# GLA on one Trainium2 core: both directions' states stacked into one 128-row product, decay factors made three levels ahead, decayed queries loaded per chunk

## The chip, the core and the metric

The kernel runs on one core of one Trainium2 chip. A core has a matrix engine (TensorE: PE in the rows, its weight loads PEld), a vector engine (VectorE: DVE), a scalar engine (ScalarE: ACT), GpSimd (POOL) and SyncE (SP), whose queue issues most DMA transfers. The engines run side by side, each through its own instructions in a fixed order, and wait for one another by semaphores. Products are written to PSUM, which POOL does not read. The metric is the device time of one execution in microseconds; the median of three runs counts.

## The reference, cut to what matters

One step of a network of two mixer layers over 2,048 latent positions and 128 context positions, all in float32. The change is in the first layer's gated linear attention (GLA): 4 heads with keys of 64 and values of 128, run forwards and backwards over the positions.

```python
def gla_chunked(q, k, v, g, s0):
    ...
    def step(S, inp):
        qc, kc, vc, gc = inp
        b = jnp.cumsum(gc, axis=2)
        o_inter = jnp.einsum('bhcd,bhde->bhce', qc * jnp.exp(b), S)
        diff = b[:, :, :, None, :] - b[:, :, None, :, :]
        decay = jnp.where(causal, jnp.exp(jnp.where(causal, diff, 0.0)), 0.0)
        att = jnp.einsum('bhid,bhjd,bhijd->bhij', qc, kc, decay)
        o = o_inter + jnp.einsum('bhij,bhje->bhie', att, vc)
        b_last = b[:, :, -1:, :]
        S_new = jnp.exp(b_last)[:, :, 0, :, None] * S + jnp.einsum('bhcd,bhce->bhde', kc * jnp.exp(b_last - b), vc)
        return S_new, o
    ...
def gla_bidir(q, k, v, gf, gb, s0f, s0b):
    o_f, s_f = gla_chunked(q, k, v, gf, s0f)
    fl = lambda t: jnp.flip(t, axis=2)
    o_b, s_b = gla_chunked(fl(q), fl(k), fl(v), fl(gb), s0b)
    return o_f + fl(o_b), s_f, s_b
```

The GLA output is normalised per head, gated, put beside the output of the layer's second branch (S5), projected by `w_out`, and added to the input; the sum is normalised again for the second layer.

## The kernel before

The positions are 17 chunks of 128: 16 latent ones (0 to 15) and the context (16). The program is written in Python and a list scheduler fixes the order of every engine's instructions when it is built; that order, the pools of buffers and the PSUM banks decide who waits for whom.

The backward states need a pass from the last chunk to the first. `gla_back` makes it in an earlier stage, between products of other kinds: for each chunk it loads keys, cumulated gates `B` and values, decays the keys, transposes them and multiplies them with the values in `kv_update`, whose four products (one a head) lie in turn in the left and the right 64 columns of the array. Two DVE operations then write the next state into `sb`, which keeps all sixteen backward states on the chip. The pass that closes this stage, `glu_pass`, ends the S5 branch; its stores of `ys_d` and those of `zg_d` stand on POOL's queue.

Stage 4 (`phase4`) does the GLA chunks. `weave` runs four generators round by round: `gla_chunk(i)`, `turn(i-1)` (gates and transposes the previous chunk's output), `gla_pre(i+1)` (prepares the next chunk) and `after(i-2)` (output projection of 96 products, residual, norm for the next layer, transposes in `make_h`). The scheduler orders what they emit.

Within a chunk the decay is split by seven levels of distance (`STEPS` 64 to 1). For each, `gla_arg` has POOL subtract gates in four operations (the lines 980 to 983), ACT take the exponential, and DVE multiply with queries and keys (the tile `arg`); PE multiplies the pair head by head with 64 rows (L1058), and DVE merges the result into `att` under a mask (L1065). Levels 0 and 1 have two buffers, later ones four. `gla_pre` makes levels 0 to 2, and `gla_chunk` makes level `li+2` when it uses level `li`. Then PE makes the output of each head: forward state product (L1073, 64 rows), backward state product (L1074, 64 rows), attention product (L1075, 128 rows), accumulated in one bank of `psP`:

```python
if i < 16:
    nc.tensor.matmul(ot, qh[o : o + 64, 0, pr, :], sf[o : o + 64, pr], start=True, stop=False)
    nc.tensor.matmul(ot, qh[o : o + 64, 1, pr, :], self.sb[o : o + 64, i, pr], start=False, stop=False)
nc.tensor.matmul(ot, att[:, hh, pr], v[:, h * 128 : h * 128 + 128], start=i == 16, stop=True)
```

A float32 product takes two passes through the array, and shows as two instructions in the rows. The decayed queries `qh` are made on the chip from `B` and `qk`.

Of the kernel before, what the change touches and what calls it, by code (L numbers as in the profile page):

```python
# [48 lines left out]
class Kernel:  # L49
# [55 lines left out]
    def setup(self, es):  # L105
# [33 lines left out]
        self.b_d = d.tile([2, 2, 128, NT], F32, name="b_d")  # L139
        self.z_d = d.tile([16, 512, 137], F32, name="z_d")  # L140
# [749 lines left out]
    def gla_back(self, es):  # L890
# [3 lines left out]
        for i in [16] + list(range(15, 0, -1)):  # L894
# [11 lines left out]
            kv = self.kv_update(p, E, v)  # L906
            if i == 16:
                st = p.tile([128, 2, 128], F32, name="bst", tag="bst", bufs=1)
                nc.scalar.copy(st, kv)
                nc.sync.dma_start(self.o["gla"][1].rearrange("r p v -> p r v"), st)  # L910
# [30 lines left out]

    def gla_setup(self, es):
# [16 lines left out]
        self.gp = self.pool(es, "glap", 2, side="right")  # L959
        self.gs = {}  # L960
# [3 lines left out]
    def gla_arg(self, i, li):  # L964
# [10 lines left out]
        arg = self.ga["arg"][li > 1].tile([128, 2, 256], F32, name="arg", tag="arg", bufs=4 if li > 1 else 2)  # L975
# [12 lines left out]
    def gla_pre(self, i):  # L988
# [32 lines left out]
        sf = st["sf"] = self.sf  # L1021
        if i != 15:
            kv = self.kv_update(p, kh, v)
            if i == 16:
                o = p.tile([128, 2, 128], F32, name="fst", tag="sf", bufs=3)
                nc.scalar.copy(o, kv)
                nc.sync.dma_start(self.o["gla"][0].rearrange("r p v -> p r v"), o)
            else:
                self.sf = p.tile([128, 2, 128], F32, name="sf", tag="sf", bufs=3)
                for pr in range(2):  # L1030
                    V.scalar_tensor_tensor(self.sf[:, pr], sf[:, pr], eb[:, pr : pr + 1], kv[:, pr], op0=OP.mult, op1=OP.add)
        yield

    def gla_chunk(self, i, out):
# [4 lines left out]
        v, qh, sf = st["v"], st["qh"], st["sf"]  # L1039
# [736 lines left out]
```

## Time and profile before

| what | value |
|---|---|
| median of three runs | 2424.79 us (2420.01 to 2428.99) |
| the profiled execution: time, span | 2423.86 us, 2422.1 us |
| busy share of the span | PE 95%, PEld 87%, DVE 71%, ACT 41%, POOL 36% |
| mean granted TensorE clock | 0.971 of full |
| stage 4, first GLA product to last output copy | 908.8 to 1335.2 us of the span |

The profile covers one execution. Its span runs from the first to the last instruction; 1.8 us lie around it. Busy shares are means over stages that have different limits, so the stage of the change is read by itself. A granted clock of 1.00 is TensorE's upper level (2.4 GHz), 0.50 the lower (1.2 GHz); a value between is a mean over a stretch with both.

### The profile page before, as it was taken

What the parts mean: (1) busy time and instruction counts of PE and PEld (TensorE: products, weight loads), DVE (VectorE), ACT (ScalarE), POOL (GpSimd) and SP (SyncE); (2) the same over time, 40 slices, a digit from 0 to 9 for tenths busy, and PEclk for the clock granted to TensorE, in tenths of its full rate; (3) what the DMA queues carried; (4) which work ended last, traced back from release to release, by engine and by line L of the source; (5) the groups of instructions that cost most, each with busy time, mean ns of one, the idle gap of its engine ahead of it and who ended that gap; (6) DMA issues with size and microseconds to landing.
All of it is one profiled execution on the core that took longest, in us unless ns stands there. A gap on an engine that the chain in (4) does not pass through costs nothing.

```text
span 2422.1 us, 47150 instructions
## 1 busy us (share of the span) xinstructions
PE 2295.5 (95%) x17521; PEld 2110.7 (87%) x17521; DVE 1720.3 (71%) x3932; ACT 986.2 (41%) x2365; POOL 872.9 (36%) x1328
## 2 busy tenths in 40 slices
PE   7998998999999986999999999999999998999998
PEld 4987887777787875888888999999999997999998
DVE  5998689999976776888888675556344336676765
ACT  4553532222244453445554532233122115565653
POOL 4017047777612227666765022211001102222221
PEclk9999999999999995989999999999999998999999
DMA  8442552233269873333433642245124213222221
GB/s 303 153 141 79 170 159 78 80 82 96 81 202 315 294 242 112 122 105 114 124 118 99 192 135 79 79 134 169 50 73 122 68 56 113 88 88 88 89 70 57
DMA packets 313174, 303.92 MB, mean 125 GB/s; under 512 B 43696, under 2 KB 264464, under 8 KB 312944
## 3 DMA queue, kind: packets, MB, share of 16 engines
q1 hardware_dynamic: 255072, 227.70, 31.6%
q10 hardware_dynamic: 48112, 42.38, 5.4%
q0 software_dynamic: 9760, 30.83, 3.5%
q8 instruction: 138, 2.26, 0.4%
q14 instruction: 92, 0.75, 0.1%
HBM read 212.43 MB, written 88.39 MB: 124 GB/s over the span
## 4 chain that ended last, share of the span: by engine, by line
PE 53%; DVE 7%; issue 5%; DMA 4%; POOL 2%; ACT 2%; SPq 0%; ACTq 0%; POOLq 0%; DVEq 0%
PE psW L100 7%; PE psW L102 7%; PE psW L101 7%; PE psD L100 6%; PE psD L102 6%; PE psD L101 6%; PE psW L1487 2%; PE psW L1440 2%; PE psT L1475 2%; PE psP L1058 2%; PE psP L1075 1%; PE psP L1073 1%; DVE hq L1065 1%; DVE arg L985 1%; DVE yT L1103 1%
## 5 line engine op out<-in xcount | busy, mean ns | idle before, releaser
L100 PE MATMUL psD<-slot,yT 128*128 128x256 f32 x1088 | 316.4, 292 | 2.4 <-ACT yT L1102 2.4
L102 PE MATMUL psD<-slot,yT 128*128 128x256 f32 x1088 | 314.0, 292 | 0.4 <-DVE yT L1103 0.4
L101 PE MATMUL psD<-slot,yT 128*128 128x256 f32 x1088 | 311.2, 287 | 0.0
L101 PE MATMUL psW<-hq,slot 128*128 128x272 f32 x1024 | 293.0, 288 | 0.0
L102 PE MATMUL psW<-hq,slot 128*128 128x272 f32 x1024 | 292.9, 287 | 0.0
L100 PE MATMUL psW<-hq,slot 128*128 128x272 f32 x1024 | 289.1, 287 | 0.0
L101 PE MATMUL psD<-hq,slot 128*128 128x272 f32 x768 | 227.8, 297 | 14.5 <-DVE hq L230 14.5
L100 PE MATMUL psD<-hq,slot 128*128 128x272 f32 x768 | 230.0, 301 | 9.4 <-ACT fo L791 8.2
L102 PE MATMUL psD<-hq,slot 128*128 128x272 f32 x768 | 228.5, 298 | 0.0
L100 PEld LDWEIGHTS psD<-slot,yT 128*128 128x128 f32 x1088 | 208.0, 191 | 9.9 <-ACT yT L1102 2.8
L101 PEld LDWEIGHTS psD<-slot,yT 128*128 128x128 f32 x1088 | 208.1, 191 | 2.1
L102 PEld LDWEIGHTS psD<-slot,yT 128*128 128x128 f32 x1088 | 205.7, 191 | 4.3 <-issue 1.3
L102 PEld LDWEIGHTS psW<-hq,slot 128*128 128x128 f32 x1024 | 193.1, 189 | 0.0
L101 PEld LDWEIGHTS psW<-hq,slot 128*128 128x128 f32 x1024 | 192.5, 188 | 0.0
L100 PEld LDWEIGHTS psW<-hq,slot 128*128 128x128 f32 x1024 | 190.6, 188 | 0.0
L101 PEld LDWEIGHTS psD<-hq,slot 128*128 128x128 f32 x768 | 147.5, 192 | 25.4 <-DVE hq L230 19.2
L100 PEld LDWEIGHTS psD<-hq,slot 128*128 128x128 f32 x768 | 147.9, 193 | 19.5 <-ACT fo L791 10.2
L102 PEld LDWEIGHTS psD<-hq,slot 128*128 128x128 f32 x768 | 147.8, 193 | 8.2 <-issue 8.2
L1449 DVE CUSTOM_DVE_ANT_0 sc<-psW,amask,sink 128x512 f32<-128x512 f32 (+1 forms) x128 | 93.6, 732 | 82.5 <-PE psT L1475 75.3
L984 ACT ACTIVATE arg<-arg 128x512 f32<-128x512 f32 x119 | 75.2, 632 | 134.1 <-POOL arg L983 129.5
L1452 ACT ACTIVATE sc<-sc,nm 128x512 f32<-128x512 f32 (+1 forms) x128 | 90.9, 710 | 85.8 <-DVE nm L1451 71.9
L245 ACT ACTIVATE hf<-psT,msh,msc 128x128 f32<-128x128 f32 x272 | 100.6, 463 | 49.3 <-PE psT L241 49.3
(378 smaller groups left out, 6653.3 us busy)
## 6 DMA issues: line engine op xcount, KB each, us to landing
wst<-h_d SPq DMA_DIRECT2D x136, 272.0 KB
wada<-in_w_ada_dram SPq DMA_DIRECT2D x32, 512.0 KB
h_d<-hf SPq DMA_DIRECT2D x17, 512.0 KB
x_d<-x ACTq DMA_DIRECT2D x17, 512.0 KB
h_d<-hf ACTq DMA_DIRECT2D x17, 512.0 KB
wst<-h_d SPq DMA_DIRECT2D x34, 256.0 KB
qf<-qa_d SPq DMA_DIRECT2D x34, 256.0 KB
hq<-x_d SPq DMA_DIRECT2D x17, 512.0 KB
```

Of the source, the lines that this page charges most:

```text
L100: mm(out, lh, rh, start=start, stop=False)
L101: mm(out, lh, rl, start=False, stop=False)
L102: mm(out, ll, rh, start=False, stop=stop)
L245: nc.scalar.activation(f[:, k, :], pt[:, j, :], AF.Identity, bias=sh, scale=sc)
L984: nc.scalar.activation(arg, arg, AF.Exp, scale=0.0625)
L985: nc.vector.tensor_tensor(arg, arg, qk.rearrange("p j r t -> p j (r t)"), op=OP.mult)
L1058: nc.tensor.matmul(pv[:, hh, pr, :], ak[o : o + 64, pr, :], aq[o : o + 64, pr, :], start=True, stop=True)
L1440: nc.tensor.matmul(out, r32(qs[:, j, h]), kk, start=j == 0, stop=j == 1)
L1449: V.tensor_tensor_reduce(sv, ps, mask, 1.0, sk[:, h : h + 1], op0=OP.add, op1=OP.max, accum_out=m)
L1452: nc.scalar.activation(sv, src, AF.Exp, bias=nm[:, h : h + 1], accum_out=sm[:, h : h + 1])
L1475: nc.tensor.transpose(pt[:, c, :], t[:, 128 * c : 128 * c + 128], self.ident)
L1487: nc.tensor.matmul(po[kv][:, j % 2], r32(VV[:, b, kv]), r32(t[:, x, :, c, :]), start=c + x == 0, stop=c + x == nb)
```

## The change

State and query of both directions are stacked: forward in partitions 0 to 63, backward in 64 to 127, so that one product with 128 rows takes the place of the two with 64. For this the backward states go to memory (`sb_d`) in `gla_back` and come back into the lower half of `sf` (`state`); `qh` (the gates) and `qq` (the queries) are loaded in stacked form at the first step of `gla_pre`, in six transfers; `kv_update` puts all four heads into one column half; `next_state` multiplies on POOL and adds on DVE. `gla_arg` runs three levels ahead with six buffers. The norm of a tile of `after` shares the reciprocal root with the next GLA chunk (`xrow`, `rows`), is scaled on ACT, and its transposes come a chunk later; `x1` has three buffers. The 16 KB a partition of `sb` are gone.

```diff
-            kv = self.kv_update(p, E, v)
+            kv = self.kv_update(p, E, v, 64)
...
-            eb = p.tile([128, 2], F32, name="beb", tag="beb")
-            nc.scalar.activation(eb, B[:, :, 0], AF.Exp, scale=0.0625)
-            for pr in range(2):
-                nc.vector.scalar_tensor_tensor(
-                    self.sb[:, i - 1, pr], self.sb[:, i, pr], eb[:, pr : pr + 1], kv[:, pr], op0=OP.mult, op1=OP.add
-                )
+            eb = p.tile([128, 2, 2], F32, name="beb", tag="beb")
+            for hh in range(2):
+                nc.scalar.activation(eb[64:128, :, hh], B[64 * hh : 64 * hh + 64, :, 0], AF.Exp, scale=0.0625)
+            nst = p.tile([128, 4, 128], F32, name="bs", tag="bs", bufs=2)
+            self.next_state(p, slice(64, 128), nst, st, eb, kv)
+            st = nst
+            nc.gpsimd.dma_start(self.sb_d[i - 1], st[64:128])
...
-    def kv_update(self, p, kd, v):
+    def next_state(self, p, o, dst, src, eb, kv):
+
+        t = p.tile([128, 4, 128], F32, name="dst", tag="dst", bufs=1)
+        e = eb.rearrange("p a b -> p (a b)")[o].unsqueeze(2).to_broadcast([64, 4, 128])
+        self.nc.gpsimd.tensor_tensor(t[o], src[o], e, op=OP.mult)
+        self.nc.vector.tensor_tensor(dst[o], t[o], kv, op=OP.add)
+
+    def kv_update(self, p, kd, v, o):
...
-        kv = self.bank("T", (128, 2, 128))
+        kv = self.bank("T", (128, 4, 128))[o : o + 64]
         for h in range(4):
-            pr, o = h // 2, 64 * (h % 2)
+            pr, c = h // 2, 64 * (h % 2)
             nc.tensor.matmul(
-                kv[o : o + 64, pr, :],
-                kt[:, pr, o : o + 64],
-                v[:, h * 128 : h * 128 + 128],
-                start=True,
-                stop=True,
-                tile_position=(0, o),
+                kv[:, h], kt[:, pr, c : c + 64], v[:, h * 128 : h * 128 + 128], start=True, stop=True, tile_position=(0, o)
             )
         return kv
...
-        arg = self.ga["arg"][li > 1].tile([128, 2, 256], F32, name="arg", tag="arg", bufs=4 if li > 1 else 2)
+        arg = self.ga["arg"][li > 1].tile([128, 2, 256], F32, name="arg", tag="arg", bufs=6 if li > 1 else 2)
...
+        if i < 16:
+            if i == 0:
+                self.state(0)
+                nc.sync.dma_start(self.sf[0:64], a["s0"][0])
+            st["sf"] = self.sf
         v = st["v"] = self.ga["v"].tile([128, 512], F32, name="v", tag="v", bufs=1)
         nc.sync.dma_start(v, self.v_d[ts, :])
+        if i < 16:
+
+            qh = st["qh"] = p.tile([128, 4, 128], F32, name="qh", tag="qh", bufs=2)
+            qq = p.tile([128, 4, 128], F32, name="qq", tag="qq", bufs=2)
+            for d in range(2):
+                o = slice(64 * d, 64 * d + 64)
+                nc.sync.dma_start(qq[o], self.qk_d[0:256, ts].rearrange("(h k) t -> k h t", k=64))
+                for r in range(2):
+                    nc.sync.dma_start(qh[o, 2 * r : 2 * r + 2], self.b_d[r, d, :, ts].rearrange("(q k) t -> k q t", k=64))
...
-        qh, st["att"] = (qa[:, 512 * j : 512 * j + 512].rearrange("p (a b c) -> p a b c", a=2, b=2) for j in range(2))
-        st["qh"] = qh
-        nc.scalar.activation(qh, B, AF.Exp, scale=0.0625)
-        eb = p.tile([128, 2], F32, name="eb", tag="eb")
-        V.tensor_copy(eb, qh[:, 0, :, 127])
-        V.tensor_tensor(qh, qh, qk[:, 0:1].to_broadcast([128, 2, 2, 128]), op=OP.mult)
+        st["att"] = qa[:, 0:512].rearrange("p (a b c) -> p a b c", a=2, b=2)
+        if i < 16:
+
+            qh = st["qh"]
+            eb = p.tile([128, 2, 2], F32, name="eb", tag="eb")
+            nc.scalar.activation(eb[0:64].rearrange("p a b -> p (a b)"), qh[0:64, :, 127], AF.Exp, scale=0.0625)
+            nc.scalar.activation(qh, qh, AF.Exp, scale=0.0625)
+            V.tensor_tensor(qh, qh, qq, op=OP.mult)
...
-        sf = st["sf"] = self.sf
+        self.gla_arg(i, 3)
         if i != 15:
-            kv = self.kv_update(p, kh, v)
+            kv = self.kv_update(p, kh, v, 0)
...
             else:
-                self.sf = p.tile([128, 2, 128], F32, name="sf", tag="sf", bufs=3)
-                for pr in range(2):
-                    V.scalar_tensor_tensor(self.sf[:, pr], sf[:, pr], eb[:, pr : pr + 1], kv[:, pr], op0=OP.mult, op1=OP.add)
+                self.state(i + 1)
+                self.next_state(p, slice(0, 64), self.sf, st["sf"], eb, kv)
         yield
+
+    def state(self, i):
+
+        self.sf = self.gp.tile([128, 4, 128], F32, name="sf", tag="sf", bufs=3)
+        self.nc.sync.dma_start(self.sf[64:128], self.a["s0"][1] if i == 15 else self.sb_d[i])
...
-            if 2 < li + 2 < 8:
-                self.gla_arg(i, li + 2)
+            if 3 < li + 3 < 8:
+                self.gla_arg(i, li + 3)
...
-            o = 64 * hh
             ot = po[:, hh, pr]
             if i < 16:
-                nc.tensor.matmul(ot, qh[o : o + 64, 0, pr, :], sf[o : o + 64, pr], start=True, stop=False)
-                nc.tensor.matmul(ot, qh[o : o + 64, 1, pr, :], self.sb[o : o + 64, i, pr], start=False, stop=False)
+                nc.tensor.matmul(ot, qh[:, h], st["sf"][:, h], start=True, stop=False)
             nc.tensor.matmul(ot, att[:, hh, pr], v[:, h * 128 : h * 128 + 128], start=i == 16, stop=True)
...
+        ss, n = self.ss, 5 if self.xrow else 4
         for h in range(4):
-            pr, hh = h // 2, h % 2
             junk = p.tile([128, 128], BF16, name="oj", tag="oj", bufs=1)
-            nc.scalar.activation(junk, y[:, pr, hh], AF.Square, accum_out=ss[:, pr, hh : hh + 1])
-        rs = self.rsqrt(p, "ors", ss, [128, 2, 2], 128.0)
-        nc.gpsimd.tensor_tensor(y, y, rs.unsqueeze(3).to_broadcast([128, 2, 2, 128]), op=OP.mult)
+            nc.scalar.activation(junk, y[:, h // 2, h % 2], AF.Square, accum_out=ss[:, h : h + 1])
+        rs = self.rsqrt(p, "ors", ss[:, 0:n], [128, n], 128.0)
+        if self.xrow:
+            self.xrow += (rs[:, 4:5],)
+        self.ss = p.tile([128, 5], F32, name="oss", tag="oss", bufs=2)
+        rh = rs[:, 0:4].rearrange("p (r h) -> p r h", r=2).unsqueeze(3).to_broadcast([128, 2, 2, 128])
+        nc.gpsimd.tensor_tensor(y, y, rh, op=OP.mult)
...
-            x = p.tile([128, 1024], F32, name="x1", tag="x1", bufs=2)
+            x = p.tile([128, 1024], F32, name="x1", tag="x1", bufs=3)
             nc.sync.dma_start(x, self.x_src(i))
             if i == 16:
                 gB[0] = self.gate_rows(p, 0, 1)
             yield from self.out_proj(p, yTs.pop(i), ws, gB[0], x)
-            ss = p.tile([128, 1], F32, name="xss", tag="xss", bufs=2)
+            nc.scalar.dma_start(self.x1_d[ts, :], x)
+            rows()
+
             junk = p.tile([128, 1024], BF16, name="sqj", tag="ot", bufs=2)
-            nc.scalar.activation(junk, x, AF.Square, accum_out=ss)
-            nc.scalar.dma_start(self.x1_d[ts, :], x)
-            rs = self.rsqrt(p, "rs1", ss, [128, 1], 1024.0)
-            V.tensor_scalar(x, x, rs, None, op0=OP.mult)
+            nc.scalar.activation(junk, x, AF.Square, scale=float(np.sqrt(0.125)), accum_out=self.ss[:, 4:5])
+            self.xrow = (i, x)
+            if i == 16:
+                rows()
+            yield
+
+        def rows():
+
+            if not self.xrow:
+                return
+            i, x, *rs = self.xrow
+            rs = rs[0] if rs else self.rsqrt(p, "ors", self.ss[:, 4:5], [128, 1], 128.0)
+            nc.scalar.activation(x, x, AF.Copy, scale=rs)
             h, _ = self.make_h(1, 1 if i == 16 else 0, x, two)
-            nc.scalar.dma_start(self.h1_d[:, :, ts], h)
-            yield
+            nc.scalar.dma_start(self.h1_d[:, :, i * 128 : (i + 1) * 128], h)
+            self.xrow = None
...
-                c = self.pool(eR, "glac", 1, side="left")
-                self.sb = c.tile([128, 16, 2, 128], F32, name="sb")
-                self.sf = c.tile([128, 2, 128], F32, name="sf0")
-                self.nc.sync.dma_start(self.sb[:, 15], a["s0"][1])
-                self.nc.sync.dma_start(self.sf, a["s0"][0])
```

In the order of the instructions the change shows at three places that matter here. First, on PE, in a chunk of the steady part, from the first attention product L1075 on (L1073 and L1074 are the two state products, L1058 the products of the next levels):

```order
L1075 MATMUL psP<-v,hq 128x128
L1073 MATMUL psP<-sf,hq 128x128
L1074 MATMUL psP<-sb,hq 128x128
L1075 MATMUL psP<-v,hq 128x128
L1073 MATMUL psP<-sf,hq 128x128
L1074 MATMUL psP<-sb,hq 128x128
L1075 MATMUL psP<-v,hq 128x128
L1073 MATMUL psP<-sf,hq 128x128
L1074 MATMUL psP<-sb,hq 128x128
L1075 MATMUL psP<-v,hq 128x128
L1058 MATMUL psP<-arg 128x128 x4
```

and of the change, the same place (there L1099 is the stacked state product, L1100 the attention product, L1085 the product of a level, L937 a transpose of the keys):

```order
L1100 MATMUL psP<-v,hq 128x128
L1099 MATMUL psP<-sf,qh 128x128
L937 MATMUL psT<-ident,kh 128x128 x2
L1100 MATMUL psP<-v,hq 128x128
L1099 MATMUL psP<-sf,qh 128x128
L1100 MATMUL psP<-v,hq 128x128
L1099 MATMUL psP<-sf,qh 128x128
L1100 MATMUL psP<-v,hq 128x128
L1085 MATMUL psP<-arg 128x128 x4
```

The heads' 64-row products are gone, and with them the alternation of 64 and 128 rows within the group. From the first instruction that writes `psP` to the last, 64 products L1073 and 64 L1074 have become 64 L1099, and the neighbouring PE instructions differ in tiling (64 rows; 128 rows by 64 columns, L932; the whole array) 352 times before and 249 times in the change; from the end of chunk 6 to the end of chunk 16 it is 228 and 160 times.

Second, on POOL, about the handover from `glu_pass` to stage 4. Before, where the last stores of `ys_d` and `zg_d` stand:

```order
L180 DMA gate_d<-bb 2x512
L866 DMA ys_d<-gzs 128x272 x4
L812 DMA zg_d<-fo 128x272
L866 DMA ys_d<-gzs 128x272 x3
L812 DMA zg_d<-fo 128x272
L866 DMA ys_d<-gzs 128x272
L1005 TENSOR_TENSOR kh<-B 128x256
L980 TENSOR_TENSOR arg<-B 128x8x16
L981 TENSOR_TENSOR arg<-B 128x8x16
L982 TENSOR_TENSOR arg<-B 128x8x16
L983 TENSOR_TENSOR arg<-B 128x8x16
L980 TENSOR_TENSOR arg<-B 128x16x8
```

and of the change, where the key decay `kh` of chunk 0 stands:

```order
L929 TENSOR_TENSOR dst<-bs,beb 64x512
L813 DMA zg_d<-fo 128x272
L922 DMA sb_d<-bs 64x512
L867 DMA ys_d<-gzs 128x272
L1026 TENSOR_TENSOR kh<-B 128x256
L987 TENSOR_TENSOR arg<-B 128x8x16
L988 TENSOR_TENSOR arg<-B 128x8x16
L989 TENSOR_TENSOR arg<-B 128x8x16
L990 TENSOR_TENSOR arg<-B 128x8x16
L987 TENSOR_TENSOR arg<-B 128x16x8
L988 TENSOR_TENSOR arg<-B 128x16x8
L989 TENSOR_TENSOR arg<-B 128x16x8
```

Before, `kh` and the levels 2 to 6 of chunk 0 come behind the last of these stores; now they stand among them, with 28 stores of `ys_d` and `zg_d` still behind `kh`, and all seven levels of chunk 0 and one of chunk 1 ahead of the last store. The rows L929 and L922 are the new multiplication and store of `gla_back`.

Third, on SP, one chunk's transfers in the steady part, before:

```order
L1150 DMA zg<-zg_d 128x4x128
L1108 DMA ysl<-ys_d 128x4x128
L1000 DMA v<-v_d 128x512
L998 DMA B<-b_d 128x2x128 x2
L1164 DMA x_14081<-in_xs_dram 128x1024
L997 DMA qk<-qk_d 128x2x128 x2
```

and in the change:

```order
L1021 DMA qh<-b_d 64x2x128
L1012 DMA v<-v_d 128x512
L1021 DMA qh<-b_d 64x2x128 x3
L1059 DMA sf<-sb_d 64x512
L1019 DMA qq<-qk_d 64x4x128 x2
L1005 DMA B<-b_d 128x2x128 x2
L1193 DMA x_13137<-in_xs_dram 128x1024
L1004 DMA qk<-qk_d 128x2x128 x2
```

where two rows for `zg` and `ysl` stand near these as before: 15 transfers a chunk in place of 8.

## Rows read from the trace of the kernel before

**Rows 1.** Busy time of each engine by stretch (columns in its first row).

```profile
core 0: us, PE busy (x) PEld busy (x) DVE busy (x) ACT busy (x) POOL busy (x), PEclk, DMA share, GB/s
735.00:902.00 167.00, 165.65 (x1264) 137.40 (x1263) 122.14 (x257) 84.52 (x197) 44.97 (x79) 1.00 0.88 288
902.00:908.80 6.80, 0.01 (x1) 0.01 (x1) 5.43 (x13) 4.09 (x9) 1.31 (x3) 0.86 0.41 123
908.80:945.40 36.60, 23.66 (x130) 18.72 (x130) 21.39 (x37) 13.18 (x24) 27.45 (x50) 0.59 0.47 150
945.40:994.70 49.30, 44.31 (x316) 37.93 (x316) 38.26 (x84) 18.53 (x44) 32.31 (x62) 0.77 0.19 59
994.70:1095.90 101.20, 96.71 (x782) 84.77 (x782) 86.32 (x196) 49.38 (x125) 66.36 (x124) 0.93 0.40 124
1095.90:1335.20 239.30, 238.45 (x1984) 208.92 (x1985) 202.55 (x479) 119.16 (x299) 154.86 (x283) 1.00 0.36 112
```

**Rows 2.** POOL in order of time at the handover.

```profile
913.23 1.15 POOL L1005 TENSOR_TENSOR kh<-B 128x256 f32<-128x256 f32 x1 [3.36 <-ACT hq L1062]
...
946.61 0.61 POOL L980 TENSOR_TENSOR arg<-B 128x128 f32<-128x128 f32 x1 [6.47 <-PE psP L1058]
```

**Rows 3.** Chain that ended last, chunk 10: start us, us, what.

```profile
1186.41 0.59 PE psT L932 x8
...
1188.97 0.22 PE psP L1075 x2
1189.19 0.41 PE psP L1073 x2
1189.61 0.22 PE psP L1074 x2
1189.83 0.42 PE psP L1075 x2
```

**Rows 4.** The same view at the end of chunk 16.

```profile
1334.27 0.89 PE psP L1075 x8
```

**Rows 5.** The same view, one head of chunk 0.

```profile
941.62 0.72 PE psP L1073 x2
942.34 0.43 PE psP L1074 x2
942.77 0.72 PE psP L1075 x2
```

**Rows 6.** Instruction groups on POOL, 908.8 to 994.7 us.

```profile
L983 POOL TENSOR_TENSOR arg<-B 128x128 f32<-128x128 f32 x25 | 13.9, 556 | 0.0
...
L972 POOL TENSOR_TENSOR q<-qk 128x256 f32<-128x256 f32 x4 | 4.2, 1062 | 0.0
L1005 POOL TENSOR_TENSOR kh<-B 128x256 f32<-128x256 f32 x5 | 4.0, 807 | 3.4 <-ACT hq L1062 3.4
L1084 POOL TENSOR_TENSOR gy<-gy,rsy 128x512 f32<-128x512 f32 x2 | 2.8, 1380 | 1.7 <-DVE rsy L94 1.7
```

**Rows 7.** Transfers issued by SP, in order of time.

```profile
1051.87 0.88 SPq L998 DMA_DIRECT2D B<-b_d  x2
```

**Rows 8.** Instruction groups of all engines, 1095.9 to 1335.2 us.

```profile
L980 POOL TENSOR_TENSOR arg<-B 128x128 f32<-128x128 f32 x64 | 34.5, 538 | 66.5 <-PE psP L1058 61.3 <-DVE rst L93 3.5 <-DVE rsy L90 1.1
...
L1170 ACT ACTIVATE sqj<-x 128x1024 bf16<-128x1024 f32 x10 | 10.6, 1057 | 23.7 <-DVE x L1128 23.7
L1173 DVE TENSOR_SCALAR x<-x,rsy 128x1024 f32<-128x1024 f32 x10 | 8.8, 879 | 0.0
...
L93 DVE TENSOR_TENSOR rst<-rst,rsv 128x1 f32<-128x1 f32 x29 | 6.1, 211 | 0.7
```

**Rows 9.** Instruction groups on POOL, 735 to 902 us.

```profile
L866 POOL DMA_DIRECT2D ys_d<-gzs x30 | 16.4, 547 | 53.3 <-DVE gzs L865 51.1 <-issue 2.0
L812 POOL DMA_DIRECT2D zg_d<-fo x24 | 13.2, 549 | 56.4 <-DVE fo L811 45.0 <-DMA bb<-in_b_ada_dram 8.6 <-DMA bB<-b_d 2.7
...
L982 POOL TENSOR_TENSOR arg<-B 128x128 f32<-128x128 f32 x2 | 0.8, 396 | 0.0
```

More of the change, by code (lines that the diff above doesn't have):

```diff
@@ L139, in setup @@
         self.b_d = d.tile([2, 2, 128, NT], F32, name="b_d")
+        self.sb_d = d.tile([15, 64, 4, 128], F32, name="sb_d")
         self.z_d = d.tile([16, 512, 137], F32, name="z_d")
@@ L905, in gla_back @@
             nc.vector.tensor_tensor(E, E, k, op=OP.mult)
-            kv = self.kv_update(p, E, v)
+            kv = self.kv_update(p, E, v, 64)
             if i == 16:
-                st = p.tile([128, 2, 128], F32, name="bst", tag="bst", bufs=1)
-                nc.scalar.copy(st, kv)
-                nc.sync.dma_start(self.o["gla"][1].rearrange("r p v -> p r v"), st)
+                fin = p.tile([128, 4, 128], F32, name="bs", tag="bs", bufs=2)
+                nc.scalar.copy(fin[64:128], kv)
+                nc.sync.dma_start(self.o["gla"][1].rearrange("r (q k) v -> k (r q) v", q=2), fin[64:128])
+                st = p.tile([128, 4, 128], F32, name="bs", tag="bs", bufs=2)
+                nc.sync.dma_start(st[64:128], a["s0"][1])
                 yield
                 continue
-            eb = p.tile([128, 2], F32, name="beb", tag="beb")
-            nc.scalar.activation(eb, B[:, :, 0], AF.Exp, scale=0.0625)
-            for pr in range(2):
-                nc.vector.scalar_tensor_tensor(
-                    self.sb[:, i - 1, pr], self.sb[:, i, pr], eb[:, pr : pr + 1], kv[:, pr], op0=OP.mult, op1=OP.add
-                )
-            yield
-    def kv_update(self, p, kd, v):
+            eb = p.tile([128, 2, 2], F32, name="beb", tag="beb")
[5 more added lines that the diff above has]
+            nc.gpsimd.dma_start(self.sb_d[i - 1], st[64:128])
+            yield
+    def next_state(self, p, o, dst, src, eb, kv):
[4 more added lines that the diff above has]
+    def kv_update(self, p, kd, v, o):
         nc = self.nc
@@ L959, in gla_setup @@
         self.gp = self.pool(es, "glap", 2, side="right")
+        self.ss, self.xrow = self.gp.tile([128, 5], F32, name="oss", tag="oss", bufs=2), None
         self.gs = {}
@@ L1020, in gla_pre @@
         yield
-        sf = st["sf"] = self.sf
+        self.gla_arg(i, 3)
         if i != 15:
-            kv = self.kv_update(p, kh, v)
+            kv = self.kv_update(p, kh, v, 0)
             if i == 16:
-                o = p.tile([128, 2, 128], F32, name="fst", tag="sf", bufs=3)
-                nc.scalar.copy(o, kv)
-                nc.sync.dma_start(self.o["gla"][0].rearrange("r p v -> p r v"), o)
-            else:
-                self.sf = p.tile([128, 2, 128], F32, name="sf", tag="sf", bufs=3)
-                for pr in range(2):
-                    V.scalar_tensor_tensor(self.sf[:, pr], sf[:, pr], eb[:, pr : pr + 1], kv[:, pr], op0=OP.mult, op1=OP.add)
+                o = p.tile([128, 4, 128], F32, name="fst", tag="dst", bufs=1)
+                nc.scalar.copy(o[0:64], kv)
+                nc.sync.dma_start(self.o["gla"][0].rearrange("r (q k) v -> k (r q) v", q=2), o[0:64])
+            else:
+                self.state(i + 1)
+                self.next_state(p, slice(0, 64), self.sf, st["sf"], eb, kv)
         yield
+    def state(self, i):
+        self.sf = self.gp.tile([128, 4, 128], F32, name="sf", tag="sf", bufs=3)
+        self.nc.sync.dma_start(self.sf[64:128], self.a["s0"][1] if i == 15 else self.sb_d[i])
     def gla_chunk(self, i, out):
@@ L1038, in gla_chunk @@
         st = self.gs[i]
-        v, qh, sf = st["v"], st["qh"], st["sf"]
+        v, qh = st["v"], st.get("qh")
         att = st["att"]
@@ L1077, in gla_chunk @@
         V.tensor_copy(y.rearrange("p r h v -> p h r v"), po)
-        ss = p.tile([128, 2, 2], F32, name="oss", tag="oss")
+        ss, n = self.ss, 5 if self.xrow else 4
         for h in range(4):
-            pr, hh = h // 2, h % 2
             junk = p.tile([128, 128], BF16, name="oj", tag="oj", bufs=1)
-            nc.scalar.activation(junk, y[:, pr, hh], AF.Square, accum_out=ss[:, pr, hh : hh + 1])
-        rs = self.rsqrt(p, "ors", ss, [128, 2, 2], 128.0)
-        nc.gpsimd.tensor_tensor(y, y, rs.unsqueeze(3).to_broadcast([128, 2, 2, 128]), op=OP.mult)
+            nc.scalar.activation(junk, y[:, h // 2, h % 2], AF.Square, accum_out=ss[:, h : h + 1])
[5 more added lines that the diff above has]
+        nc.gpsimd.tensor_tensor(y, y, rh, op=OP.mult)
         out[i] = y.rearrange("p r h v -> p (r h) v")
@@ L1723, in prep @@
         "rmask": c_(np.broadcast_to((np.arange(256) % 128 != 0).astype(f), (128, 256))),
-        "s0": c_(n["state_gla"][0, 0].reshape(2, 2, 128, 128).transpose(0, 2, 1, 3)),
+        "s0": c_(n["state_gla"][0, 0].transpose(0, 2, 1, 3)),
         "lmask": lmask,
```

## Prediction

> **What bounds the kernel now.** I read the kernel by stretches first [rows 1]. From 1095.9 to 1335.2 us (chunks 7 to 16 of stage 4) PE is busy for 238.45 of 239.3 us at a granted clock of 1.00, and DVE for 202.55, POOL for 154.86, ACT for 119.16: PE alone is full, and a chunk takes 23.9 us because its PE instructions take that long. The stretch with `gla_back` and the products of `glu_pass`, 735 to 902 us, is full on PE too (165.65 of 167.0). Between them lies another case: at the handover (902.0 to 908.8) PE does nothing, and through the first three chunks, 908.8 to 994.7, which take 85.9 us, it is busy for 67.97 us at granted clocks of 0.59 and 0.77, that is, for much of the time at its lower level of 1.2 GHz. The clock had been 1.00 until the pause; it fell when PE paused and came back only once PE was full.
>
> Why PE is starved there POOL's own order of time shows [rows 2]: the key decay `kh` of chunk 0 starts at 913.23, after the last glu product, and every level from the third on comes behind it. At the end of chunk 0 POOL itself stands still for 6.47 us until PE has read an `arg` (L1058): with four buffers POOL can't run ahead. So there are two things to price: PE's work where PE is full, and POOL's lead where it isn't.
>
> What PE's work costs I read in the chain of one steady chunk [rows 3]. Two passes of L1075 behind others of their own kind take 0.22 us, 0.111 each; two passes of L1074 behind L1073, both 64 rows, the same 0.22. But L1073 behind L1075 takes 0.41 and L1075 behind L1074 0.42: each change between 64 and 128 rows adds 0.20. A head costs 0.41 + 0.22 + 0.42 = 1.05 us.
>
> **Steady part, chunks 7 to 16.** Passes: nine chunks with state (16 has none) lose eight 64-row passes each (four heads, two passes): 72 x 0.111 = -8.0 us. Changes of tiling: the order counts 228 before and 160 now, 68 x 0.20 = -13.6. `kv_update` pays: its eight passes took 0.59 us [rows 3], while eight 128-row passes take 0.89 [rows 4]. With 0.20 for the change of tiling in front, 0.59 leaves 0.39, the time of four passes: products in the two column halves went side by side. In one half they can't, so eight calls cost 4 x 0.111 = 0.445 more each: +3.6. Sum -18.0, from 239.3 to 221.3 us, 22.1 a chunk. The bounds: -8 if a change between 128x64 and the whole array is dearer than I think or the waits fill what is won, -22 if `kv_update` costs nothing.
>
> The Trainium skill's TensorE: Matmul & The Clock Gate, Part 3: Packing small matmuls, has small products in distinct row or column groups run at once in the array. By it the stacking gives up something: forward and backward products put in different row halves could have overlapped. The trace agrees with it for the pairs of L932; for L1073 and L1074, which use the same 64 rows of a head, it shows two full costs one behind the other. By the rule alone the steady part would gain 10 us, by the row 18.
>
> **Chunks 3 to 6.** The same rate plus 2 us, since the granted clock in this stretch is 0.93: 101.2 becomes 4 x 22.1 + 2 = 90.4, -10.8. If the clock still falls as often, -4; if not at all, -13.
>
> **`gla_back`.** 16 calls of `kv_update` lose the same pairing, 64 products whose two passes cost one slot more between them: 64 x 0.111 = +7.1 us in a full stretch. Between 0 (weights, not columns, set their pace) and 9. Its new multiplication and store on POOL lie beside about 10 us of PE work a step (165.65 us over 17 steps); POOL was busy for 44.97 of 167.0 us there [rows 1].
>
> **First three chunks.** At the lower clock a head costs 0.72 + 0.43 + 0.72 = 1.87 us [rows 5]; three products become two without a change, 4 passes of about 0.22, 0.89. But the main thing is that all seven levels, `q` and `kh` of chunk 0 and one level of chunk 1 now stand on POOL among the last stores of glu and are made there. From PE's first GLA product (t = 0) POOL still has to make 13 levels, six of chunk 1 and seven of chunk 2. Group means in the same stretch [rows 6]: 13 levels x 4 x 0.556 = 28.9; two `q` 2.1, two `kh` 1.6, two `gy` 2.8, three state multiplications at most 1.38 each (L1084, the same 512 elements a row, on 128 partitions; at least 0.81, `kh`) 4.1: 39.5. Behind its last level come exponentials, masking, products at a low clock and the copy, some 8 us as an estimate (four heads at 0.89, and as much again and a little for the rest): 48 us. PE's own work here, counted from the new order at 0.111 a pass and 0.20 a change, is 8.6, 9.6 and 19.7 us a chunk (the output projection begins only in the third), 38 us at the upper clock, so POOL still decides. From 85.9 to 48 is -38. Bounds: 38 (PE full from the start) and 78 (only the products at the lower clock are saved, -8).
>
> The queries and gates of chunk 0 are loaded late, behind the last stores. SP issues two transfers in 0.88 us [rows 7]; eight of them take 3.5 us, and with somewhat more than that again for the last store and the load to land, the first stacked query is there near t = 8, about when PE comes to the state products of chunk 0.
>
> **What I cost at nothing, and its cover.** Busy times a chunk are a tenth of those of the ten chunks [rows 1]. In 22.1 us POOL has 15.5 plus a state multiplication of at most 1.4, and it waited 61.3 us for PE in ten chunks [rows 8]. DVE loses the scaling of x (0.88) and a root of its own, eleven operations of about 0.21, from 20.3 to about 17. ACT takes the scaling at the price of its nearest row, L1170, 1.06: 11.9 to 13. SP has 15 issues, 6.7 us. If the cover is gone, on POOL first, each of these counts in full, 1.4 us a chunk. The end of the stage has one more tile to transpose (eight passes of 0.11) and a scaling of 1.06 behind a root: +2.
>
> **Sum.** +7.1 - 38 - 10.8 - 18.0 + 2 = -57.7. The profiled execution took 2423.9 (span 2422.1 and 1.8 around it), 0.9 under the median of 2424.8: 2424.8 - 57.7 = 2367 us.
>
> **Rivals.** First, POOL becomes the bound of the steady part. For: its level operations take 0.538 beside a busy DVE [rows 8] and 0.396 in the glu stretch [rows 9], so one slows the other, and the new loads and the faster PE press both. Against: DVE gets less work. POOL's 15.5 + 1.4 reaches 22.1 when 28 level operations each grow by 0.19, to 0.73. Then the period stays near 24 and chunks 3 to 16 gain nothing: 2367 + 28.8, about 2395.
> The Trainium skill's GPSIMD Engine Reference, 1. Specifications, says that GpSimd shares its SBUF interfaces with VectorE. The trace's 0.396 and 0.538 agree.
>
> Second, the lead doesn't come: levels wait for something else (the late queries, a load of `B`), the first chunks stay at 78 us. 2367 + 30 = 2397; 2404 if chunks 3 to 6 then gain only 4.
>
> Third, the 64-row products already run side by side with their neighbours in a way that the chain hides, as those of `kv_update` do. Then only the changes of tiling are won: +8 in the steady part and +6 before it, 2381. Against it stand the 0.41 and 0.22 of one head [rows 3]. The packing rule of the Trainium skill named above is the one that speaks for it.
>
> Fourth, better than forecast: PE full from the first chunk, 38 us there, and `kv_update` at no cost: 2367 - 10 - 11, about 2346; with DVE's relief some us less.
>
> Fifth, the other side: `kh` on POOL now stands ahead of 28 stores of `ys_d` and `zg_d`. If it has to wait for a load or for memory, these stores wait, the buffers `gzs` and `fo` fill, and the glu products stop, us for us. 54 stores in 167 us [rows 9] make 28 of them 87 us of glu work: that is the most it can hold back. It decides from 58 us on; in full, 2367 + 87 = 2454. Against: `kh` before waited for memory that glu held, and here it must have memory of its own.
>
> **How the numbers follow.** Forecast 0.56, POOL bound 0.12, no lead 0.11, overlap already 0.04, better 0.05, stores held back 0.07, and 0.05 that the gains meet waits I don't see and the time stays. I predict 2367 us. Apart from the last two and half of the better case all lie between 2342 and 2405. Half a per cent, 12 us, is about what a measurement of this kernel can tell from no change: faster 0.88, same 0.05, slower 0.07.
>
> **What would show it.** Of the changed kernel I'd read: the state product L1099 at 0.22 for two passes and no 0.41 within a head; L932's successor at 0.89 or more for eight passes; `kh` of chunk 0 and all its levels ahead of the first GLA product; chunks 0 to 2 in about 48 us with a granted clock above 0.8; steady chunks at 22.1 us with PE above 97%. Wrong would be: POOL busy above 95% of the steady part, a POOL wait of some 10 us ahead of `kh` with PE idle in glu, or PE waiting for `sf`, `qh` or `qq` in the first chunk.

## The result, and the profile after

The changed kernel took 2439.74 us (median of four runs, 2437.47 to 2440.7) against 2424.02 of the kernel before: a ratio of 1.0063, with a 95% interval of 1.0042 to 1.0083. It is slower by 0.6%, where 2.4% faster was forecast. The profiled spans are 2438.5 and 2422.1 us.

The stretches of the changed kernel, with the columns of [rows 1]: the glu stage to its last product, the handover, chunk 0, chunks 1 and 2, chunks 3 to 6, chunks 7 to 16.

```profile
735.00:918.90 183.90, 173.96 (x1268) 145.30 (x1266) 135.57 (x244) 92.17 (x213) 81.18 (x128) 0.98 0.85 275
918.90:927.20 8.30, 0.00 (x0) 0.01 (x1) 6.91 (x16) 4.12 (x9) 2.15 (x4) 0.76 0.64 205
927.20:950.30 23.10, 17.24 (x103) 14.30 (x103) 18.95 (x26) 9.95 (x20) 18.70 (x33) 0.57 0.57 162
950.30:997.20 46.90, 37.84 (x276) 33.82 (x276) 41.59 (x69) 17.05 (x43) 34.60 (x64) 0.82 0.48 144
997.20:1103.80 106.60, 96.42 (x781) 86.38 (x782) 81.48 (x145) 50.40 (x123) 66.93 (x128) 0.94 0.42 128
1103.80:1346.90 243.10, 226.01 (x1912) 203.59 (x1911) 192.36 (x347) 127.23 (x315) 149.22 (x282) 0.98 0.43 131
```

Against [rows 1], stretch by stretch (the tail runs from the last output copy to the end of the span, 1086.9 us before):

| stretch | before, us | after, us | difference | forecast |
|---|---|---|---|---|
| up to the first GLA product | 908.8 | 927.2 | +18.4 | +7.1 |
| chunks 0 to 2 | 85.9 | 70.0 | -15.9 | -38 |
| chunks 3 to 6 | 101.2 | 106.6 | +5.4 | -10.8 |
| chunks 7 to 16 | 239.3 | 243.1 | +3.8 | -18.0 |
| tail | 1086.9 | 1091.6 | +4.7 | +2 |

The last row of the profile holds the surprise. PE's work did shrink, from 238.45 to 226.01 us, but the stretch grew: PE now stands for 17 us of it, where it stood for one. No engine has become full: POOL is busy for 149 of 243 us, DVE for 192. So it is a wait, and the view of PE's waits in that stretch names the place (what waited, for what; us in total, times, longest):

```profile
PE psP L1085 <- DVE rst L92: 6.2, 2, 5.3
PE psP L1085 <- DVE rst L93: 5.4, 4, 3.0
PE psP L1085 <- DVE rsy L94: 3.0, 2, 2.5
```

L92 to L94 are the small operations of the reciprocal root. The level products L1085 don't need them; what they do need of DVE, the merge L1092 of an earlier level, stands among them in DVE's order. The longest of these waits, in order of time over all engines, shows what held DVE:

```profile
1185.38 0.21 ACT L1036 ACTIVATE eb<-qh 64x4 f32<-64x4 f32 x1 [2.80 <-DMA qh<-b_d]
1185.71 1.03 POOL L929 TENSOR_TENSOR dst<-sf,eb 64x512 f32<-64x512 f32 x1 [5.08 <-issue]
...
1186.71 0.40 POOL L987 TENSOR_TENSOR arg<-B 128x128 f32<-128x128 f32 x1
1186.75 4.30 DVE L1038 TENSOR_TENSOR qh<-qh,qq 128x512 f32<-128x512 f32 x1 [2.68 <-ACT qh L1037]
...
1190.05 0.45 POOL L988 TENSOR_TENSOR arg<-B 128x128 f32<-128x128 f32 x1
1190.46 0.84 POOL L989 TENSOR_TENSOR arg<-B 128x128 f32<-128x128 f32 x1
1190.97 0.71 DVE L1092 COPY_PREDICATED hq<-mk,psP 128x512 f32<-128x512 uint8 x1
...
1191.83 1.01 PE L1085 MATMUL psP<-arg 64*128 64x128 f32 x6 [5.26 <-DVE rst L92]
```

Read it from the top. The gates `qh` land late; ACT waits 2.80 us for them and makes `eb`, the decay of the state. POOL has stood for 5.08 us at the state multiplication L929, which reads `eb`. Once it is through, three levels are waiting behind it, and POOL runs them without a break, an operation every 0.4 us. DVE starts its multiplication L1038 into this run and needs 4.30 us, where its shortest instance in this trace takes 0.67. It ends during POOL's eleventh operation. Then comes the merge L1092, then PE.

The gates are late because their buffer comes free late. `qh` has two buffers, so a chunk's gates can be loaded only after the state products L1099 of the chunk two before have read theirs. In the trace SP issues the first of these transfers 0.03 us behind the end of the last such L1099 in seven of fourteen chunks, and 0.85 to 3.50 us behind it in the others; ACT starts `eb` another 3.9 to 7.0 us later. A third buffer was not tried.

Stage 4 of the changed kernel has fifteen DVE operations above 1.3 us, 39.7 us in all; in the kernel before the longest takes 1.22. The groups of instructions from 1103.8 to 1346.9 us give the sums (busy, mean ns of one, idle before):

```profile
L1038 DVE TENSOR_TENSOR qh<-qh,qq 128x512 f32<-128x512 f32 x8 | 14.3, 1784 | 8.8 <-ACT qh L1037 8.8
L1099 PE MATMUL psP<-sf,qh 128*128 128x128 f32 x72 | 14.0, 276 | 0.0
L943 PE MATMUL psT<-v,kt 128*64 128x128 f32 x64 | 8.7, 279 | 0.0
...
L929 POOL TENSOR_TENSOR dst<-sf,eb 64x512 f32<-64x512 f32 x7 | 8.4, 1204 | 12.1 <-issue 5.1 <-ACT eb L1036 3.4 <-DVE sf L930 2.1
```

The two PE groups are what was forecast (9 chunks with eight passes, 8 calls of `kv_update`); L1038 takes 1.78 us in the mean, and POOL idles for 12.1 us ahead of L929.

### The profile page after: what moved, and what is told of

Same layout as the page of the kernel before. It is cut to its first block, busy times and chain, and to the rows that moved or that the text cites. A ratio compares the mean times of both kernels' runs of the same rounds, so it can differ in the third digit from the quotient of the medians.

```text
span 2438.5 us, 46982 instructions
## 1 busy us (share of the span) xinstructions
PE 2279.0 (93%) x17393; PEld 2107.8 (86%) x17393; DVE 1721.8 (71%) x3713; ACT 1006.2 (41%) x2412; POOL 905.9 (37%) x1373
## 4 chain that ended last, share of the span: by engine, by line
PE 51%; DVE 7%; DMA 5%; issue 5%; ACT 3%; POOL 2%; SPq 1%; ACTq 0%; DVEq 0%; POOLq 0%
PE psW L100 7%; PE psW L101 7%; PE psW L102 7%; PE psD L100 6%; PE psD L102 6%; PE psD L101 5%; PE psW L1480 3%; PE psW L1527 3%; PE psT L1515 2%; PE psP L1085 2%; DMA qh<-b_d 1%; ACT hf L246 1%; DVE hq L1092 1%; DVE arg L992 1%; PE psT L943 1%
## 5 line engine op out<-in xcount | busy, mean ns | idle before, releaser
L100 PE MATMUL psD<-hq,slot 128*128 128x272 f32 x768 | 229.4, 300 | 10.4 <-ACT fo L792 10.4
L1489 DVE CUSTOM_DVE_ANT_0 sc<-psW,amask,sink 128x512 f32<-128x512 f32 (+1 forms) x128 | 93.7, 732 | 82.8 <-PE psT L1515 75.7
L1085 PE MATMUL psP<-arg 64*128 64x128 f32 x952 | 94.6, 315 | 43.8 <-DVE rst L93 13.1
L1085 PEld LDWEIGHTS psP<-arg 64*128 64x128 f32 x952 | 70.5, 202 | 63.0 <-issue 27.7
```

The lines of the kernel that those rows point to most:

```text
L100: mm(out, lh, rh, start=start, stop=False)
L1085: nc.tensor.matmul(pv[:, hh, pr, :], ak[o : o + 64, pr, :], aq[o : o + 64, pr, :], start=True, stop=True)
L1489: V.tensor_tensor_reduce(sv, ps, mask, 1.0, sk[:, h : h + 1], op0=OP.add, op1=OP.max, accum_out=m)
```

## The experiments

Theory 1 is this chain: late gates, POOL held at L929, its levels in one bunch, DVE held up, PE waiting. Theory 2, the rival: six buffers and three levels of lead let POOL run in bunches, whatever starts them. Ratios are to the kernel before, measured on the same chip, with 95% intervals.

**Where the state is made.** Two edits take L929's wait away, one by an earlier source, one by another engine; a third undoes the lead.

```diff
-nc.scalar.activation(eb[0:64].rearrange("p a b -> p (a b)"), qh[0:64, :, 127], AF.Exp, scale=0.0625)
+for hh in range(2):
+    nc.scalar.activation(eb[0:64, :, hh], B[64 * hh : 64 * hh + 64, 0, :, 127], AF.Exp, scale=0.0625)
```

> The change with one edit: the decay eb of the forward state is made from the tile B, which is loaded early, not from the stacked gates qh. Theory 1 (the state multiplication on GpSimd waits for the late gates, the levels behind it then run in one bunch and hold up VectorE, and PE waits for VectorE): GpSimd no longer waits for eb, VectorE operations above 1.3 us (15 of them in stage 4 of the change, 29 us above their usual 0.7) nearly vanish, chunks 7 to 16 go from 243 to about 230 us, and the time falls by 15 to 25 us, to about 2420. Theory 2 (six buffers and three levels of lead let GpSimd run in bunches, whatever starts them): no change beyond 5 us, 2435 to 2440.

2425.5 us, ratio 1.0003 (0.9992 to 1.0013): 14 less than the change. In chunks 7 to 16 (columns of [rows 1]) PE's idle time falls from 17.1 to 8.2 us; in stage 4 the long DVE operations go from fifteen to eight, the longest from 4.42 to 3.14 us.

```profile
1103.40:1336.70 233.30, 225.14 (x1916) 202.23 (x1917) 182.48 (x347) 127.14 (x320) 150.30 (x282) 0.99 0.46 136
```

```diff
-self.next_state(p, slice(0, 64), self.sf, st["sf"], eb, kv)
+e = eb.rearrange("p a b -> p (a b)")
+for h in range(4):
+    V.scalar_tensor_tensor(self.sf[0:64, h], st["sf"][0:64, h], e[0:64, h : h + 1], kv[:, h], op0=OP.mult, op1=OP.add)
```

> The change with the forward state of stage 4 multiplied and added on VectorE (four operations a chunk), nothing of it on GpSimd. Theory 1: GpSimd has nothing that waits for the gates, the long VectorE operations go, about 2420, less if VectorE itself now waits for the gates. Theory 2: no change beyond 5 us, or slower by VectorE's extra 1 us a chunk, 2435 to 2450.

2415.0 us, 0.9955 (0.9937 to 0.9973): 25 less than the change, and faster than before it. Its chunks 7 to 16, in the columns of [rows 1]:

```profile
1092.90:1318.50 225.60, 218.87 (x1898) 198.36 (x1895) 179.99 (x367) 126.63 (x313) 142.06 (x275) 0.99 0.46 138
```

Two long DVE operations are left in stage 4. The forecast for this stretch had been 221.3. Of the 17.5 us by which the stretch is shorter than in the change, 10.4 are PE's idle time and 7.1 its busy time: an edit also makes the scheduler order PE's products anew, here with 141 changes of tiling against 155 (counted in the traces), and the mean granted clock is 0.99 in place of 0.98.

```diff
-    bufs=6 if li > 1 else 2
+    bufs=4 if li > 1 else 2
-        self.gla_arg(i, 3)
-            if 3 < li + 3 < 8:
-                self.gla_arg(i, li + 3)
+            if 2 < li + 2 < 8:
+                self.gla_arg(i, li + 2)
```

> The change with the old lead: levels two ahead, four buffers, three levels made in the preparation. Theory 1: the wait of the state multiplication stays, the bunches are shorter by a level or two of four operations; stage 4 is about the same or loses what the lead gave its first chunks: 2435 to 2450. Theory 2: the bunches go and the time falls to about 2420.

2450.95 us, 1.0104 (1.0083 to 1.0124): slower still. With the old lead DVE is held just as long, in fourteen operations above 1.3 us with 49.1 us in all:

```profile
1193.90 4.44 DVE L1038 TENSOR_TENSOR qh<-qh,qq 128x512 f32<-128x512 f32 x1 [2.38 <-ACT qh L1037]
```

Theory 2 falls: the bunch is there without the lead and the six buffers. The same edit on top of the state on DVE tells what the lead is worth by itself:

> The forward state on VectorE (2415 us) with the old lead: two levels, four buffers. What is three levels of lead worth once GpSimd is free of the state? If the gain of the first three chunks (85.9 to 68 us) comes from the lead: they take 75 to 85 us again and the time is 2422 or more. If it comes from chunk 0's work being made in the glu stage, whatever the lead: 68 to 72 us, and 2415 to 2418.

2418.6 us, 0.9956 (0.9941 to 0.9972). Chunks 0 to 2 take 65.8 us, so their gain is not the lead's. Chunks 7 to 16 take 231.8 us against 225.6, nearly all of it PE's busy time (224.79 against 218.87), but the ratios of the two runs are alike (0.9956, 0.9955), and the next run, which has the lead, takes 230.8 us there: no worth of the lead is shown. Then the first two edits together:

> The forward state on VectorE and eb made from B, both edits together. Theory 1: with the state on VectorE its four operations still wait for the late gates; with eb from B they don't, so PE's remaining waits in stage 4 (25 us, of them 7 in chunks 7 to 16) shrink by some 5: about 2410, against 2415 for the state on VectorE alone. If the lateness of eb no longer matters once GpSimd is free of it: 2415 within 3.

2414.4 us, 0.9944 (0.9922 to 0.9965). Once POOL is free of the state, the time of `eb` doesn't count.

**PE's work in `kv_update`.** The products go back into both column halves, and the add moves them to the stacked rows.

```diff
-kv = self.bank("T", (128, 4, 128))[o : o + 64]
-    nc.tensor.matmul(kv[:, h], kt[:, pr, c : c + 64], ..., tile_position=(0, o))
+kv = self.bank("T", (128, 2, 128))
+    nc.tensor.matmul(kv[c : c + 64, pr], kt[:, pr, c : c + 64], ..., tile_position=(0, c))
```

> The change with the products of kv_update back in alternating column halves; the add that follows is split in two and moves them to the stacked rows. Theory 1: PE is full in the stage of gla_back and so gains there what the pairing saves, 16 calls x 0.43 = 7 us (1.02 us for eight passes back to 0.59); stage 4 is bound by waits, so its 16 calls give little: about 2432. If the kv products are the whole loss of both stages: 14 us, about 2426. If PE's work doesn't count in either stage: 2440.

2436.6 us, 1.0042 (1.0028 to 1.0057): 3 less by the medians, with intervals that overlap. In the profile the gain is not where it was expected. In the glu stage the first GLA product comes no earlier (930.0 us, 927.2 in the change), and PE idles for 24.8 us from 715 us to there in place of 20.0; stage 4, which was to gain little, takes 412.3 us in place of 419.7. On top of the two edits of the state:

> The forward state on VectorE, eb made from B, and the kv products in alternating column halves; the VectorE operations of the forward state read the half in which each head lies. Theory 1: stage 4 is now nearly full on PE, so that the pairing counts there, 16 x 0.43 = 7 us, where it gave 2 to 3 in the kernel bound by waits: about 2403. If stage 4 still follows its waits: within 3 of the two edits without it, about 2410.

2406.65 us, 0.9919 (0.9891 to 0.9946), 8 less than without the pairing, though the intervals overlap. In the profiles stage 4 takes 383.5 us, not 389.3, near the 7 us expected there; the first GLA product comes 7.6 us earlier too (920.9, not 928.5), and the tail takes back 2.8.

**The glu stage.** From 715 us to the last glu product PE waits for 11 to 16 us in all these versions, 2.6 before the change. Four runs look for the cause. The first gives `gzs` eight buffers for four:

> The forward state on VectorE, and eight buffers in place of four for gzs, the tiles whose stores stand on GpSimd's queue at the end of the glu stage. Theory H (the key decay and levels of chunk 0 on GpSimd stand ahead of these stores, the buffers stay taken, the loads into them come late and the glu products wait): the first GLA product comes some 8 to 12 us earlier than at 930, PE's idle time from 715 us to there falls from 21 to about 12, the time to about 2405. Rival (the stage is held by its memory traffic, at a share of 0.95, and by the new order elsewhere): 2415 within 3.

2421.0 us, 0.9977 (0.9963 to 0.9992): the first GLA product at 931.5, nothing gained. PE's idle time from 715 us to there did fall, from 21.3 to 13.8 us, but PE was busy for longer (202.7 us, not 193.9), so the run decides against neither of the two. The second makes the backward state on DVE as well (the edit of `next_state`, on rows 64 to 127):

> Forward and backward states multiplied and added on VectorE. If GpSimd's multiplication in gla_back holds up its queue of loads' decays and stores there, the first GLA product comes 5 us or more earlier than at 930 and the time falls to about 2409; if not, 2415 within 3.

2413.4 us, 0.9939 (0.9917 to 0.9961): PE waits 7.7 us before the handover in place of 13.0, but the first GLA product comes at 928.5, not 5 us earlier, and the time falls by less than the runs spread. With the pairing:

> Both states on VectorE, kv products in alternating halves, eb from the gates as in the change. The gains seen apart: both states on VectorE 2413, the pairing some 8 us more. Theory 1 and PE's work both count: about 2405, and a stage 4 of some 385 us against 420 of the change. If the gains are one and the same: 2412.

2402.8 us, 0.9896 (0.9879 to 0.9912), 11 less than without the pairing; here the intervals don't overlap. On it, `nc.gpsimd.dma_start(self.ys_d[bs, ts], zs)` becomes `nc.scalar.dma_start`:

> As the run before it in this call (both states on VectorE, kv products in halves), and the stores of ys_d issued by ScalarE in place of GpSimd. Theory H in its other form (what is late at the end of the glu stage is the issue of these stores behind chunk 0's work on GpSimd's queue): the first GLA product comes 5 us or more earlier and the time falls by as much. If it is not the queue: the same within 3, or slower because ScalarE waits for VectorE ahead of each store.

2406.7 us, 0.991 (0.988 to 0.994). Its profile, of the fastest of its four runs, has the first GLA product at 915.4, 6 us earlier, but the four spread over 16 us and no gain is shown.

**The norm of the rows.** On the version with both states on DVE and the pairing (2402.8 us, the expectation's "first run"), `after` gets back its own root, its scaling on DVE, its transposes in the same chunk and two buffers for `x1`, as on the minus side of the diff.

> As the first run of this call (both states on VectorE, kv products in halves), with the norm of the residual rows as before the change: its own reciprocal root and its scaling on VectorE, transposes in the same chunk, two buffers. In the change the tail behind the last copy of stage 4 takes 1091.5 us against 1086.9, and PE waits 6.4 us there for the first product of the next stage. If the later transposes cause it: the tail returns to about 1087, stage 4 loses up to 1 us a chunk to VectorE, the sum within 6 us of the first run. If memory or order causes it: the tail stays at 1091 or more, and the time is the same or up to 10 us longer.

2400.1 us, 0.9879 (0.9857 to 0.9902), the lowest of all, though the interval overlaps with that of 2402.8. The tail is 1086.8 us (1094.0 without this edit), and chunks 7 to 16 pay nothing, though DVE is busier there (without and with this edit, columns of [rows 1]):

```profile
1082.00:1307.30 225.30, 212.99 (x1889) 192.91 (x1888) 183.08 (x367) 128.10 (x314) 141.94 (x275) 1.00 0.46 137
1087.60:1313.00 225.40, 213.21 (x1889) 192.70 (x1888) 209.64 (x485) 118.27 (x306) 143.80 (x272) 1.00 0.46 140
```

What was left of the glu stage's waits was asked by tying chunk 0's gates to the last store of that stage:

```diff
+if i == 0:
+    t = p.tile([128, 1], F32, name="tie", tag="tie", bufs=1)
+    nc.sync.dma_start(t, self.ys_d[384:512, NT - 1 : NT])
+    b = B.rearrange("p d r t -> p (d r t)")
+    V.scalar_tensor_tensor(b, t.to_broadcast([128, 512]), 0.0, b, op0=OP.mult, op1=OP.add)
```

> Both states on VectorE, kv products in halves and the norm as before the change (2400 us), and chunk 0's gates tied to the last store of the glu stage, so that none of its levels, nor its key decay, is made there: 28 level operations and the decay leave the glu stage on GpSimd, with their exponentials and multiplications on ScalarE and VectorE. If chunk 0's early work is what makes PE wait in the glu stage (some 10 us in all versions against 2.6 before the change): the idle time before the handover falls to 5 us or less, the glu products end 6 to 10 us earlier, and the first three chunks take 10 to 20 us more, so the time is 2400 to 2412. If the waits come from gla_back's longer chain or the traffic: the glu end stays, and the time is 2410 to 2420.

2425.25 us, 0.9994 (0.9983 to 1.0005). Its glu stage and what follows:

```profile
735.00:904.40 169.40, 168.47 (x1289) 141.14 (x1288) 131.05 (x277) 86.76 (x205) 49.13 (x85) 1.00 0.92 304
904.40:926.20 21.80, 0.03 (x2) 0.03 (x2) 10.62 (x22) 7.65 (x16) 5.43 (x11) 0.59 0.52 161
926.20:1001.90 75.70, 61.49 (x441) 53.11 (x442) 59.92 (x118) 30.07 (x68) 61.71 (x123) 0.73 0.41 118
```

The glu products end at 904.4, not 915.2, with 3.8 us of idle time from 715 us on in place of 10.9: the early work of chunk 0 is most of what PE waits for. But chunks 0 to 2 take 75.7 us, not 65.1, so the early work gives back there what it costs. The handover, too, lasts 21.8 us in place of 9.5, but that is not all the early work: the last store is issued at 911.85 us and the gates are free at 921.6, a delay that the tie itself makes. The time expected, 2400 to 2412, was missed.

> The same 2400 us version, with the stores of ys_d issued by ScalarE. In the version with the merged norm this brought the first GLA product from 921.5 to 915.4 us, but the times spread from 2398 to 2414. If that gain is real: 2394 to 2397. If it is only a shift of waits: 2400 within 4.

2400.7 us, 0.9897 (0.988 to 0.9914): no gain of the store queue is shown here either.

## Why the prediction was wrong

**The count of PE's work was right, or nearly.** The state product takes 0.22 us for two passes and a head 0.44, as forecast. In chunks 7 to 16 PE was to be busy for 238.45 - 18.0 = 220.5 us; it was for 226.0 in the change, and for 218.9 with the state on DVE, in another order of its products. The products of the 16 calls of `gla_back`, before and after, cost 6.9 us more, where +7.1 was forecast:

```profile
L932 PE MATMUL psT<-bv,kt 128*64 128x128 f32 x128 | 10.5, 285 | 0.0
L943 PE MATMUL psT<-bv,kt 128*64 128x128 f32 x128 | 17.4, 279 | 1.5 <-ACT kt L939 1.5
```

**The step that failed: "What I cost at nothing, and its cover".** The state multiplication was priced at 1.4 us of a POOL that waits 61 us for PE, and the new loads at SP's issue time. Both prices count time on an engine, not order and not when a buffer comes free. L929 was put into a queue that PE's next levels share, and behind a transfer that waits for its buffer. Its own time is 1.20 us in the mean, inside the price; in the instance shown it held three levels, let them go at once, and DVE was held with them. Taking it off POOL gave back 25 us (27 between the profiled spans: 17.5 in chunks 7 to 16, 12.0 in chunks 3 to 6, -2 elsewhere), and chunks 3 to 16 then lie 8.5 us above their forecast, where the change lies 38.0 above it. This is none of the rivals as written: the 0.05 for waits "I don't see" names no wait. The nearest is the first, POOL as the bound through contention with DVE; it was tied to POOL being full, and POOL was busy for 61% of the stretch, its level operations at 0.50 to 0.52 us and not 0.73. (Its two prices are of two lines, L980 and L982; L982 by itself goes from 0.396 to 0.600 in the kernel before.) How much of the 25 us is POOL's wait, how much the hold on DVE and how much the new order on PE, the runs don't separate: an earlier `eb` shortens the first two (14 us).

That step is not the whole miss. Between the forecast and the measurement lie 74 us of the profiled spans: 11 up to the first GLA product, 22 in chunks 0 to 2, 38 in chunks 3 to 16 and 3 in the tail.

The Trainium skill (SBUF — State Buffer, Who interferes with whom) says that a VectorE instruction with two SBUF inputs contends with a GpSimd instruction that reads SBUF, over a shared port pair that is an exclusive lock. The trace agrees, and shows how far it can go: L1038, with two SBUF inputs, lasted through eleven instructions of POOL.

**First three chunks, -38 forecast, -15.9 measured.** The work counted was right, the clock was left out. PE is busy there for 55.1 us at mean granted clocks of 0.57 and 0.82, which is, as an estimate, 41 us of work at the upper level, against 38 counted; it started behind an idle handover at the lower level, as before the change. It idles for 14.9 us more. One wait of 5.4 us, until 961.3 us, stands behind another long DVE operation, and from 962 to 967 us the clock is 0.50 again, the lower level. About half of what was gained comes from the early levels (75.7 us without them, 65.1 with, 85.9 before the change), none of it from the longer lead. How much of the miss is the clock and how much the waits, no run separates.

**Glu stage, +7.1 forecast, +18.4 measured.** 6.9 is the pairing. PE's idle time before the handover (from 715 us) grew from 2.6 to 11.7 us and the handover from 6.8 to 8.3, together 17.5. The fifth rival had the right place, chunk 0's work among the glu work, and the wrong size: some 11 us at the glu end (904.4 against 915.2), not 58 or more, and without it the first chunks lose as much. No run shows that the kernel became slower by it.

**Chunks 3 to 6 and the tail.** The first follow the steady part (94.6 us with the state on DVE, 90.4 forecast). Of the tail's +4.7, forecast as +2, all goes with the merged norm: 1086.8 without it. The time it should save on DVE was worth nothing in chunks 7 to 16, which take 225.3 us with it and 225.4 without.

## What to carry to other kernels

Before an operation is moved to an engine with spare time, ask what it waits for and which work stands behind it there: a busy share says nothing on that. Of a new load ask when its buffer comes free. On POOL ask also what runs when the wait ends: here bunches of eight to twelve operations stood beside DVE operations of 2.4 to 4.4 us. Saved work counts only where no wait takes its place: in chunks 7 to 16 PE's work fell by 12 us and the stretch grew by 4.

## What the runs showed of the hardware

A DVE operation with both operands in SBUF (L1038, L992) that met a run of POOL operations some 0.36 to 0.41 us apart could last until the run was nearly over: 4.30 us in the change and 4.44 with the old lead, each until the eleventh of twelve. So could small ones of the reciprocal root (4.42 us for one of 128x4, at 954.9 us, until the twelfth). In other places the two engines took turns, as in the kernel before, where no DVE operation of stage 4 lasted over 1.22 us. Most long ones began during L929 or right behind it, but what decides between turns and a hold was not tried.

In the glu stage of the change two waits of PE, of 1.5 us (until 724.2 us) and 3.1 us (until 797.7), stood beside a time at the lower level: the mean granted clock is 0.91 from 720 to 740 us, 0.92 from 780 to 800 and 0.91 from 800 to 820. Two others, of 2.0 and 1.5 us (until 759.9 and 777.6), did not: it is 1.00 from 740 to 780 us. With chunk 0's work tied to the end of the stage, PE waits for 0.9 us from 735 to 904.4 us, and the mean there is 1.00; in the change it waits for 9.9 us from 735 us on, and the mean is 0.98.
